# Up-projection's values in products of 256 columns, with ScalarE's bank copies put ahead of taps and GELU

## The chip, the cores and the metric

One core of one Trainium2 chip. The metric is the device time of one execution in microseconds (us). The profile is one execution recorded by the hardware profiler. Its engines are TensorE (PE, with its weight loads shown as PEld), VectorE (DVE), ScalarE (ACT), GpSimd (POOL) and SyncE (SP, which issues the large DMAs).

## The reference

A trunk of two layers over 512 tokens of 1024 features. The change lies in the gated MLP that both layers have:

```python
def _conv_ffn(h, w_up, conv_w, conv_b, w_down):
    u = _causal_depthwise_conv(h @ w_up, conv_w) + conv_b
    gate, up = jnp.split(u, 2, axis=-1)
    return (jax.nn.gelu(gate, approximate=False) * up) @ w_down

def reference(x, p, positions, ...):
    for i in range(DEPTH):
        ...
        x = x + _conv_ffn(_rms_norm(x, ffn_norm[i]), ffn_w_up[i], ffn_conv_w[i], ffn_conv_b[i], ffn_w_down[i])
        x = x + _per_layer_embedding(x, p[i], ple_norm[i], ple_w_gate[i], ple_w_proj[i])
    return x
```

`w_up` is 1024 x 5632: the first 2816 columns are the gate, the others the values (`up`). The convolution is causal, depthwise and three taps wide. Everything is float32.

## The kernel before

**Numbers as pairs.** Each float32 operand is split into a high part of a shorter type (`float32r`) and a low part, the rest. ScalarE writes the high part (`Copy` into `wh`, or `uh`, `a`, `four`), then VectorE subtracts it to get the low part (`wl`, `ul`). For weights this is `cut` (L146 on ScalarE, L147 on VectorE) or `cut_blocks` (L822, L823); for activations `split` (L105, L106). A product then is three matmuls: high by high, high by low, low by high (`mm3`, L166 to L168; in the block products L875 to L877). Features lie on the 128 partitions, the 512 tokens along the free dimension, so a full product is 512 columns wide and fills one PSUM bank of 512 float32. Eight blocks of 128 features (`xg[0]` to `xg[7]`, pairs) make up the contraction.

**One group.** `ffn` runs over 11 groups `d` in each layer. A group computes two blocks of 128 value columns and two blocks of 128 gate columns.

The two value blocks are plain products in `value` (L950): 8 blocks of the contraction by 3 matmuls, 512 columns wide, into one bank each (`ps` of `begin`, called the late value, and `V0`). Their weights are cut by `column` (L947, with `cut`) and lie at the start of their tiles.

The two gate blocks are computed by `seven` (L860), with seven block products in place of eight: contraction, columns and tokens are each halved, weights and activations are added and subtracted beforehand (`first_forms`, `more_forms`; for the activations `operand`), and seven products of 256 tokens, 12 matmuls each, are accumulated into the right halves of banks. Their weights come from `cut_blocks`, which puts the high parts 16 and the low parts 48 elements into a tile (`BLOCKS`). What one bank has in common with another is carried over by copies of ScalarE between banks: W's left half into X and Y (L886, L887), V into `more` in SBUF (L893), Y's left half to X's right (L896) and X's right half to Y's right (L900). `seven` is a generator; each `yield` is a place where TensorE is given value products, so that a copy can be made meanwhile.

TensorE's order is written out by hand (`manual_schedule`, L1039). For a group it is:

| run | matmuls | columns | what must be there |
|---|---|---|---|
| late value, blocks 0 to 5 | 18 | 512 | weights of value 1 |
| W | 12 | 256 | `plain` |
| late value, blocks 6 and 7 | 6 | 512 | |
| V | 12 | 256 | `t13` |
| X left | 12 | 256 | copy L886 |
| Y left | 12 | 256 | copy L887, `t` |
| V0, blocks 0 to 3 | 12 | 512 | weights of value 0 |
| X right | 12 | 256 | copy L896 |
| V0, blocks 4 to 7 | 12 | 512 | |
| Y left (`last`) | 12 | 256 | copy L900, `last` |
| X right (`last`) | 12 | 256 | |

That is 48 matmuls of 512 columns and 84 of 256. In the first group, the norm's transposes stand after each half of V0.

**After the products.** Each of the four banks goes through `taps` (L923): VectorE multiplies by the norm's scale `R` (L926; for Y, which first has `more` added, L929 and L932), ScalarE makes the middle tap with the bias (L933), VectorE adds the two other taps (L935, twice). ScalarE's GELU over both gate blocks (L1064) and VectorE's product with the values (L976 or L986, in `place`) end the group. These lines of group d are traced after `prepare(d + 1)` and `begin(d + 1)`, so they run while TensorE is in group d + 1. Their order on ScalarE and VectorE isn't written out: the scheduler places them, by traced order and its own estimates. From group 4 on, earlier results are split in between (`split_one`). ScalarE and VectorE each work through their instructions in order; one that waits holds up all behind it.

**Buffers.** `wh` and `wl` have three buffers each, the raw weights (1 MB DMAs on SP's queue, two for a group) two, the banks of kind `pa` (W, V, values) four, those of kind `ps` (X, Y) four. A weight cut must wait until the product that used its buffer three cuts earlier is over.

After the last group, `down` (L1091) multiplies by `w_down`; its first cuts are traced by `pump(0)` (L1195).

Of the kernel before, what the change touches and what calls it, by code (L numbers as in the profile page):

```python
# [1 line left out]

# [1 line left out]

# [14 lines left out]
P = 128  # L19
# [36 lines left out]


BLOCKS = (16, 48)


class Kernel:
# [64 lines left out]
        t = self.wp.tile([P, 2048], F32, tag="raw", name=self.nm("raw"), bufs=2)  # L126
        return t[:, : na * nb].rearrange("p (a b) -> p a b", b=nb)

    def cut(self, rv, by):


        nc = self.nc
        na, nb = rv.shape[1:]
        parts = []
        n = 2 if na * nb > 1024 else 1
        for k in range(n):
            if by == "b":
                a, b = na, nb // n
                v = rv[:, :, k * b : (k + 1) * b]
            else:  # L140
                a, b = na // n, nb
                v = rv[:, k * a : (k + 1) * a, :]
            h, l = self.weight_tiles()
            hv = h[:, : a * b].rearrange("p (a b) -> p a b", b=b)
            lv = l[:, : a * b].rearrange("p (a b) -> p a b", b=b)
            nc.scalar.activation(hv, v, AF.Copy)  # L146
            nc.vector.tensor_tensor(lv, v, hv.bitcast(F32), ALU.subtract)  # L147
# [12 lines left out]
        return get  # L160
# [699 lines left out]
    def seven(self, od, ws, xg, forms, keep=True):  # L860
# [35 lines left out]
        nc.scalar.copy(X[:, right], Y[:, left])  # L896
        yield
        last = self.cut_blocks(od)
        product(X[:, right], t13, 1, s3)
        nc.scalar.copy(Y[:, right], X[:, right])  # L900
        yield
        product(Y[:, left], last, 1, s4)
        product(X[:, right], last, 0, tokens(1, 1))
        yield X, Y, more
# [1 line left out]
    def ffn(self, i, project, next_gain):  # L906
# [8 lines left out]
        with tc.tile_pool(name=f"ffn{i}", bufs=1) as fp:  # L915
# [4 lines left out]
            def both():  # L920
                return fp.tile([P, 2, S], F32, tag="zt", name=self.nm("zt"), bufs=2)

            def taps(y, ps, f, more=None):  # L923
                z = fp.tile([P, S], F32, tag="z", name=self.nm("z"), bufs=3)
                if more is None:
                    nc.vector.tensor_tensor(z, ps, R, ALU.mult)  # L926
                else:
                    h2 = lambda x: x.rearrange("p (u t) -> p u t", u=2)
                    nc.vector.tensor_tensor(  # L929
                        h2(z), h2(ps), more.unsqueeze(1).to_broadcast([P, 2, S // 2]), ALU.add  # L930
                    )
                    nc.vector.tensor_tensor(z, z, R, ALU.mult)  # L932
                nc.scalar.activation(y, z, AF.Identity, scale=w2[:, f : f + 1], bias=bb[:, f : f + 1])  # L933
                for tap, w in ((1, w1), (2, w0)):
                    nc.vector.scalar_tensor_tensor(  # L935
                        out=y[:, tap:], in0=z[:, : S - tap], scalar=w[:, f : f + 1], in1=y[:, tap:],
                        op0=ALU.mult, op1=ALU.add,
                    )
# [6 lines left out]
                return out  # L945

            def column(raw, c):  # L947
                return self.cut(raw[:, :, c * P : (c + 1) * P], "b")

            def value(w, ps, k0, k1):  # L950
                for k in range(k0, k1):
                    self.mm3(ps, w(k, 0, P), xg[k], start=k == 0, stop=k == ND - 1)

            def prepare(d):

# [82 lines left out]
            steps, w1c, w0c = ready  # L1038
            with tc.manual_schedule(engines={ET.PE}):  # L1039
                late = begin(0, steps, w1c)  # L1040
                for d in range(groups):
                    g, y = both(), both()
                    next(steps)
                    V0 = self.pa()
                    value(w0c, V0, 0, ND // 2)
                    if d == 0:
                        self.end_norm()
                    next(steps)
                    value(w0c, V0, ND // 2, ND)
                    if d == 0:  # L1050
                        R = self.spread()
                    X, Y, more = next(steps)
                    rest = late

                    if d + 1 < groups:
                        steps, w1c, w0c = prepare(d + 1)
                        late = begin(d + 1, steps, w1c)
                    else:
                        split_acts()
                    rest(y)  # L1060
                    taps(y[:, 0], V0, NF + 2 * d)
                    taps(g[:, 0], X, 2 * d)
                    taps(g[:, 1], Y, 2 * d + 1, more)
                    nc.scalar.activation(g, g, AF.Gelu)  # L1064
                    place(d, g, y)
                    if 4 <= d < groups - 1:
                        split_one(d - 4)
            self.begin_norm(mine)
            finish = lambda m: self.advance(m, next_gain)
            if i == 1:  # L1070
# [14 lines left out]
            self.down(i, acts, down_forms, both, work, finish)  # L1085
            if i == 0:
                self.end_norm()
            else:
                self.ple1(fp)

    def down(self, i, acts, forms, both, work, finish):  # L1091


        nc, tc = self.nc, self.tc
# [96 lines left out]
        with tc.manual_schedule(engines={ET.PE}):  # L1191
            with tc.high_priority(offset=300):
                for _ in range(2):
                    load(loads.pop(0))
                pump(0)  # L1195
            for t, (u, name, k0, k1, s) in enumerate(plan):
                own = u not in banks
                if own:
# [778 lines left out]
```

## Time and profile before

| | |
|---|---|
| median of 3 runs | 1205.41 us (1204.26 to 1207.05) |
| the profiled execution: time, span | 1205.4 us, 1203.6 us |
| first value product of layer 0, of layer 1 | at 178.36 us, at 798.47 us |
| first product of the down-projection after each | at 406.80 us, at 1027.25 us |
| TensorE's granted clock, both stretches | 1.00 |

The two up-projections with their block products take 228.4 and 228.8 us, 38% of the span. A matmul's record in the trace lasts longer than the distance to the next one's start, since matmuls are pipelined; what TensorE really spends is read from start to start. In the view of lines and in the timeline, each row names engine, line, operation, tiles written and read (buffer numbers left out) and shape; in brackets stands how long its engine had been idle and what ended that.

### The profile page before, as it was taken

Reading aid. Unit: us, or ns where it says so; the run is one execution under the profiler, and the core shown is the slowest. Engines: PE = TensorE matmul, PEld = TensorE weight load, DVE = VectorE, ACT = ScalarE, POOL = GpSimd, SP = SyncE. Lnnn points to the kernel's source line nnn. Section 1 sums busy time; section 2 is a strip of 40 time slices with the busy share of each in tenths; the row PEclk is TensorE's granted clock in tenths of the full one; section 3 lists DMA queues with packets and bytes.
Section 4 is the critical chain, followed back from the end, with each engine's and each line's share of the span. In section 5 each row is a group of like instructions: output and inputs, shape, how many; then the busy total and the mean of one; then the engine's idle time right before and its main releaser. Section 6 shows DMA issues by size and latency. Waiting matters only on the chain.

```text
span 1203.6 us, 17728 instructions
## 1 busy us (share of the span) xinstructions
PE 1196.3 (99%) x7018; PEld 1036.0 (86%) x7018; DVE 968.4 (80%) x1543; ACT 665.5 (55%) x1093; POOL 44.7 (4%) x64
## 2 busy tenths in 40 slices
PE   9999999999999999999999999999999999999998
PEld 8877789998899889888988988889998898888887
DVE  6786687899999987746679876678999998978595
ACT  7466565656465643534563654555565555645374
POOL 2600000000000000000100000000000000000000
PEclk9999999999999999999999999999999999999999
DMA  7232222424232332232322222323242423322601
GB/s 222 74 102 72 74 71 72 139 71 138 74 122 89 119 121 89 93 105 82 111 93 70 74 68 70 106 74 102 72 139 70 141 70 124 131 88 97 210 1 70
DMA packets 111127, 117.61 MB, mean 98 GB/s; under 512 B 2840, under 2 KB 106322, under 8 KB 111044
## 3 DMA queue, kind: packets, MB, share of 16 engines
q1 hardware_dynamic: 109680, 115.35, 29.4%
q8 instruction: 55, 0.90, 0.3%
q0 software_dynamic: 560, 0.42, 0.3%
q10 hardware_dynamic: 804, 0.70, 0.2%
q14 instruction: 28, 0.23, 0.1%
HBM read 114.37 MB, written 2.10 MB: 97 GB/s over the span
## 4 chain that ended last, share of the span: by engine, by line
PE 82%; DVE 12%; DMA 2%; ACT 2%; issue 1%; ACTq 0%; DVEq 0%
PE ps L166 14%; PE ps L167 14%; PE ps L168 14%; PE pa L167 5%; PE pa L166 5%; PE pa L168 5%; PE ps L875 4%; PE ps L877 4%; PE ps L876 4%; DVE zt L935 3%; DMA raw<-in_ffn_w_up_dram 2%; DVE wl L823 2%; PE pa L875 2%; PE pa L877 2%; PE pa L876 2%; DVE wl L147 1%
## 5 line engine op out<-in xcount | busy, mean ns | idle before, releaser
L146 ACT ACTIVATE wh<-raw 128x1024 fp32r<-128x1024 f32 (+4 forms) x154 | 152.3, 991 | 141.7 <-PE ps L167 101.3
L147 DVE TENSOR_TENSOR wl<-raw,wh 128x1024 fp32r<-128x1024 f32 (+4 forms) x154 | 175.1, 1138 | 52.9 <-ACT wh L146 52.3
L822 ACT ACTIVATE wh<-raw 128x1024 fp32r<-128x1024 f32 x78 | 82.8, 1061 | 120.6 <-DVE raw L847 65.4
L935 DVE SCALAR_TENSOR_TENSOR zt<-z,vfa,zt 128x510 f32<-128x510 f32 (+1 forms) x176 | 130.7, 744 | 11.7 <-ACT zt L933 11.2
L823 DVE TENSOR_TENSOR wl<-raw,wh 128x1024 fp32r<-128x1024 f32 x78 | 95.3, 1222 | 24.3 <-ACT wh L822 24.2
L933 ACT ACTIVATE zt<-z,vfb 128x512 f32<-128x512 f32 x88 | 71.0, 809 | 29.4 <-DVE four L986 12.8
L166 PE MATMUL ps<-b,wh 128*128 128x512 f32 x192 | 76.7, 399 | 0.0
L167 PE MATMUL ps<-b,wh 128*128 128x512 f32 x192 | 75.1, 391 | 0.0
L168 PE MATMUL ps<-b,wl 128*128 128x512 f32 x192 | 75.0, 391 | 0.0
L167 PE MATMUL pa<-b,wh 128*128 128x512 f32 x176 | 69.0, 392 | 0.0
L167 PE MATMUL pa<-a,wh 128*128 128x512 f32 x176 | 69.0, 392 | 0.0
L166 PE MATMUL pa<-a,wh 128*128 128x512 f32 x176 | 69.0, 392 | 0.0
L166 PE MATMUL pa<-b,wh 128*128 128x512 f32 x176 | 69.0, 392 | 0.0
L168 PE MATMUL pa<-a,wl 128*128 128x512 f32 x176 | 68.4, 389 | 0.0
L168 PE MATMUL pa<-b,wl 128*128 128x512 f32 x176 | 68.4, 389 | 0.0
L875 PE MATMUL ps<-four,wh 128*128 128x256 f32 x232 | 65.3, 282 | 0.7 <-ACT ps L896 0.7
L877 PE MATMUL ps<-four,wl 128*128 128x256 f32 x232 | 64.4, 278 | 0.0
L876 PE MATMUL ps<-four,wh 128*128 128x256 f32 x232 | 64.2, 277 | 0.0
L166 PE MATMUL ps<-a,wh 128*128 128x512 f32 x160 | 63.6, 398 | 0.0
L167 PE MATMUL ps<-a,wh 128*128 128x512 f32 x160 | 62.4, 390 | 0.0
L168 PE MATMUL ps<-a,wl 128*128 128x512 f32 x160 | 62.4, 390 | 0.0
L166 PE MATMUL ps<-uh,wh 128*128 128x512 f32 x128 | 50.3, 393 | 0.0
(472 smaller groups left out, 3495.6 us busy)
## 6 DMA issues: line engine op xcount, KB each, us to landing
raw<-in_ffn_w_up_dram SPq DMA_DIRECT2D x44, 1024.0 KB, 5.1
raw<-in_ffn_w_down_dram SPq DMA_DIRECT2D x13, 1024.0 KB, 4.8
raw<-in_hy_w_in_dram SPq DMA_DIRECT2D x8, 1024.0 KB, 5.2
raw<-in_gla_w_in_dram SPq DMA_DIRECT2D x8, 1024.0 KB, 5.1
raw<-in_ffn_w_down_dram SPq DMA_DIRECT2D x8, 768.0 KB, 4.2
raw<-in_ple_w_gate_dram SPq DMA_DIRECT2D x6, 1024.0 KB, 4.7
raw<-in_hy_w_out_dram SPq DMA_DIRECT2D x16, 256.0 KB, 4.0
raw<-in_gla_w_out_dram SPq DMA_DIRECT2D x4, 1024.0 KB, 4.8
```

Of the source, the lines that this page charges most:

```text
L146: nc.scalar.activation(hv, v, AF.Copy)
L147: nc.vector.tensor_tensor(lv, v, hv.bitcast(F32), ALU.subtract)
L166: mm(out, lh, rh, start=start, stop=False, **kw)
L167: mm(out, lh, rl, start=False, stop=False, **kw)
L168: mm(out, ll, rh, start=False, stop=stop, **kw)
L822: nc.scalar.activation(h, src, AF.Copy)
L823: nc.vector.tensor_tensor(l, src, h.bitcast(F32), ALU.subtract)
L875: mm(out, wh, xh, start=first and j == 0, stop=False, **kw)
L876: mm(out, wh, xl, start=False, stop=False, **kw)
L877: mm(out, wl, xh, start=False, stop=j == ND // 2 - 1, **kw)
L933: nc.scalar.activation(y, z, AF.Identity, scale=w2[:, f : f + 1], bias=bb[:, f : f + 1])
L935: nc.vector.scalar_tensor_tensor(out=y[:, tap:], in0=z[:, : S - tap], scalar=w[:, f : f + 1], in1=y[:, tap:], op0=ALU.mult, op1=ALU.add,)
```

## The change

Four edits, of which the first three belong to the value products and their order:

1. `value` runs over the left and the right half of the tokens, 256 columns each, and over the contraction within each half: 2112 matmuls of 256 columns in place of 1056 of 512. Only the very first opens the bank's accumulation.
2. `column` puts the values' weights at the offsets of the block products (`BLOCKS`). The tiles had room for that already.
3. The copies L896 and L900 are handed out by the generator, and `issue_after` orders later instructions of ScalarE behind them: GELU, product and split of group d - 1 (now `close`, traced one step later, behind L896's copy of group d), the late value's taps (behind L900's copy), and the down-projection's first cut (behind the last L900 copy).
4. `taps` orders Y's multiply by `R` (L932) on VectorE behind the low part of the last cut made by then (`rest_cut`: the second value block of the next group).

```diff
+HALVES = (slice(0, S // 2), slice(S // 2, S))
...
-            h, l = self.weight_tiles()
+            h, l = self.weight_tiles(offs)
...
-            nc.vector.tensor_tensor(lv, v, hv.bitcast(F32), ALU.subtract)
+            self.rest_cut = nc.vector.tensor_tensor(lv, v, hv.bitcast(F32), ALU.subtract)
...
-        nc.scalar.copy(X[:, right], Y[:, left])
-        yield
+        yield nc.scalar.copy(X[:, right], Y[:, left])
...
-        nc.scalar.copy(Y[:, right], X[:, right])
-        yield
+        yield nc.scalar.copy(Y[:, right], X[:, right])
...
-                    nc.vector.tensor_tensor(z, z, R, ALU.mult)
+                    with tc.issue_after(behind.ins) if behind else nullcontext():
+                        nc.vector.tensor_tensor(z, z, R, ALU.mult)
...
-                return self.cut(raw[:, :, c * P : (c + 1) * P], "b")
+                return self.cut(raw[:, :, c * P : (c + 1) * P], "b", BLOCKS)
...
-                for k in range(k0, k1):
-                    self.mm3(ps, w(k, 0, P), xg[k], start=k == 0, stop=k == ND - 1)
+                for c, k in itertools.product(HALVES, range(k0, k1)):
+                    self.mm3(
+                        ps[:, c], w(k, 0, P), [x[:, c] for x in xg[k]], start=c.start == 0 and k == 0,
+                        stop=k == ND - 1,
+                        skip_group_check=True,
+                    )
...
                 late = begin(0, steps, w1c)
+                close = lambda: None
                 for d in range(groups):
                     g, y = both(), both()
-                    next(steps)
+                    copied = next(steps)
+                    with tc.issue_after(copied.ins):
+                        close()
                     V0 = self.pa()
                     value(w0c, V0, 0, ND // 2)
...
-                    next(steps)
+                    copied = next(steps)
                     value(w0c, V0, ND // 2, ND)
...
-                    rest = late
+                    rest, cut = late, None
                     if d + 1 < groups:
                         steps, w1c, w0c = prepare(d + 1)
+                        cut = self.rest_cut
                         late = begin(d + 1, steps, w1c)
                     else:
                         split_acts()
-                    rest(y)
+                    with tc.issue_after(copied.ins):
+                        rest(y)
                     taps(y[:, 0], V0, NF + 2 * d)
                     taps(g[:, 0], X, 2 * d)
-                    taps(g[:, 1], Y, 2 * d + 1, more)
-                    nc.scalar.activation(g, g, AF.Gelu)
-                    place(d, g, y)
-                    if 4 <= d < groups - 1:
-                        split_one(d - 4)
+                    taps(g[:, 1], Y, 2 * d + 1, more, cut)
+
+                    def close(d=d, g=g, y=y):
+                        nc.scalar.activation(g, g, AF.Gelu)
+                        place(d, g, y)
+                        if 4 <= d < groups - 1:
+                            split_one(d - 4)
+
+                close()
...
-                pump(0)
+                with tc.issue_after(copied.ins):
+                    pump(0)
```

The built program has the same instructions as before on ScalarE, VectorE, GpSimd and SyncE, in another order on the first two within the up-projections and just behind them; GpSimd's and SyncE's orders are the same. TensorE has 1056 matmuls more, each with its weight load.

More of the change, by code (lines that the diff above doesn't have):

```diff
@@ L1 @@
-from contextlib import ExitStack
+import itertools
+from contextlib import ExitStack, nullcontext
 import numpy as np
@@ L127, in raw, with cut @@
         return t[:, : na * nb].rearrange("p (a b) -> p a b", b=nb)
-    def cut(self, rv, by):
+    def cut(self, rv, by, offs=(0, 0)):
         nc = self.nc
@@ L921, in both, with taps @@
                 return fp.tile([P, 2, S], F32, tag="zt", name=self.nm("zt"), bufs=2)
-            def taps(y, ps, f, more=None):
+            def taps(y, ps, f, more=None, behind=None):
                 z = fp.tile([P, S], F32, tag="z", name=self.nm("z"), bufs=3)
@@ L1084, in ffn @@
                 split_pair(f)
-            self.down(i, acts, down_forms, both, work, finish)
+            self.down(i, acts, down_forms, both, work, finish, copied)
             if i == 0:
@@ L1089, in ffn, with down @@
                 self.ple1(fp)
-    def down(self, i, acts, forms, both, work, finish):
+    def down(self, i, acts, forms, both, work, finish, copied):
         nc, tc = self.nc, self.tc
```

## The prediction

> **What bounds the kernel now.** I read the page's busy table first, then the chain that ended last, then the stretches of the two up-projections, and then the starts of single matmuls.
>
> ```profile
> span 1203.6 us, 17728 instructions
> PE 1196.3 (99%) x7018; PEld 1036.0 (86%) x7018; DVE 968.4 (80%) x1543; ACT 665.5 (55%) x1093; POOL 44.7 (4%) x64
> ...
> PE 82%; DVE 12%; DMA 2%; ACT 2%; issue 1%; ACTq 0%; DVEq 0%
> ```
>
> TensorE is busy for 99% of the span and makes up 82% of the chain, so only what it does between two starts can be won. Its records overlap (a matmul is booked for 0.28 or 0.40 us, yet the next one starts much sooner), so I count from start to start. These rows are the first product of each run of one group of the up-projection (columns: start, duration, engine, line, tiles). The first and last are the starts of two successive groups.
>
> ```profile
> 261.59 0.40 PE L166 MATMUL pa<-a,wh 128*128 128x512 f32 x1
> ...
> 265.69 0.28 PE L875 MATMUL pa<-a,wh 128*128 128x256 f32 x1
> ...
> 267.07 0.40 PE L166 MATMUL pa<-a,wh 128*128 128x512 f32 x1
> ...
> 268.46 0.28 PE L875 MATMUL pa<-four,wh 128*128 128x256 f32 x1
> ...
> 269.84 0.28 PE L875 MATMUL ps<-a,wh 128*128 128x256 f32 x1
> ...
> 271.20 0.28 PE L875 MATMUL ps<-four,t 128*128 128x256 f32 x1
> ...
> 272.56 0.40 PE L166 MATMUL pa<-a,wh 128*128 128x512 f32 x1
> ...
> 275.31 0.28 PE L875 MATMUL ps<-four,wh 128*128 128x256 f32 x1
> ...
> 282.18 0.40 PE L166 MATMUL pa<-a,wh 128*128 128x512 f32 x1
> ```
>
> A run of twelve 256-wide products that follows another such run takes 271.20 - 269.84 = 1.36 us, and so does the next (to 272.56): 113.3 ns for each. Steady 512-wide products stand in the projection just before the first up-projection; six of them:
>
> ```profile
> 177.00 0.39 PE L166 MATMUL ps<-b,wh 128*128 128x512 f32 x1
> ...
> 178.36 0.39 PE L166 MATMUL pa<-a,wh 128*128 128x512 f32 x1
> ```
>
> That is 1.36 us for six, 226.7 ns for each: exactly two of 113.3. So a group of 48 products of 512 and 84 of 256 should take 48 x 0.2267 + 84 x 0.1133 = 20.40 us. It takes 282.18 - 261.59 = 20.59. The missing 0.19 us stands at the changes of width: the twelve 256-wide after a 512-wide run take 267.07 - 265.69 = 1.38 instead of 1.36, the six 512-wide after that 1.39 (to 268.46) instead of 1.36, the next twelve 1.38. A change between two 256-wide runs costs nothing, although one of these also changes the kind of PSUM bank (`pa` to `ps`, at 269.84) and the other the weight pool (`wh` to `t`, at 271.20). There are eight changes of width in a group: 0.19 / 8 = 24 ns for each.
>
> Some groups take longer. The starts of the second and the last group of each layer, and of what follows the last:
>
> ```profile
> 199.83 0.40 PE L166 MATMUL pa<-a,wh 128*128 128x512 f32 x1
> 386.21 0.40 PE L166 MATMUL pa<-a,wh 128*128 128x512 f32 x1
> 406.80 0.40 PE L166 MATMUL ps<-uh,wh 128*128 128x512 f32 x1
> 819.92 0.40 PE L166 MATMUL pa<-b,wh 128*128 128x512 f32 x1
> 1005.91 0.40 PE L166 MATMUL pa<-b,wh 128*128 128x512 f32 x1
> 1027.25 0.40 PE L166 MATMUL ps<-uh,wh 128*128 128x512 f32 x1
> ```
>
> The view of waits says what the long ones wait for, first for layer 0, then for layer 1 (the weight loader runs ahead of the matmuls, so its waits are longer than what TensorE loses):
>
> ```profile
> PEld ps L875 <- ACT ps L896: 0.9, 2, 0.7
> PEld ps L875 <- ACT ps L900: 0.4, 1, 0.4
> PEld ps L875 <- ACT ps L886: 0.2, 1, 0.2
> ...
> PEld ps L875 <- ACT ps L896: 1.3, 2, 0.7
> PEld ps L875 <- ACT ps L900: 0.3, 1, 0.3
> ```
>
> All are ScalarE's copies between banks. The longest of layer 0, in ScalarE's and TensorE's order of time:
>
> ```profile
> 313.87 1.06 ACT L822 ACTIVATE wh<-raw 128x1024 fp32r<-128x1024 f32 x1
> 316.01 1.06 ACT L1064 ACTIVATE zt<-zt 128x1024 f32<-128x1024 f32 x1 [1.08 <-DVE zt L935]
> 316.98 0.37 ACT L896 COPY ps<-ps 128x256 f32<-128x256 f32 x1
> ...
> 312.87 0.28 PE L875 MATMUL ps<-four,t 128*128 128x256 f32 x1
> 314.23 0.40 PE L166 MATMUL pa<-a,wh 128*128 128x512 f32 x1
> 317.40 0.39 PE L875 MATMUL ps<-four,wh 128*128 128x256 f32 x1 [0.26 <-ACT ps L896]
> ```
>
> The product that the copy reads was issued by 314.23, yet the copy starts at 316.98: the GELU (L1064) stands ahead of it and itself waits 1.08 us for VectorE's taps. The run from 314.23 takes 3.17 us, in the quiet group 275.31 - 272.56 = 2.75.
>
> **The change part by part.**
>
> *Value products in halves.* 2 layers x 22 columns x 8 x 3 = 1056 matmuls of 512 columns become 2112 of 256, each with its own weight load as now. Work: 2112 x 113.3 - 1056 x 226.7 ns = 0. That is the lower bound of their price; the upper one is the kernel's other 256-wide row, where the weights lie unshifted in their tile, near the end of the program:
>
> ```profile
> 1196.35 0.28 PE L1372 MATMUL ps<-wh,b 128*128 128x256 f32 x1
> ...
> 1199.10 0.28 PE L1374 MATMUL ps<-four,a 128*128 128x256 f32 x1
> ```
>
> 23 starts in 2.75 us: 119.6 ns. At that price the halves would cost 2112 x 6.3 ns = +13.3 us. I take the first: the change moves the values' weights to the offsets (16 and 48 elements) of the block products, and the moving operand is the same tile that block products already read in both halves (token halves of `xg`), at 113.3.
>
> For this same place the Trainium skill (TensorE: Matmul & The Clock Gate, section Back-to-back issue gap) has a rule against the change: a warm matmul takes N / 2.4 ns plus about 2.5 ns whatever its width, so each split would add 2.5 ns, 2.6 us over 1056, and the sum below would be 1201.8. The rows above show no such fixed part: twelve of 256 and six of 512 both take 1.36 us.
>
> *Changes of width.* Within a group all eight go. From the rows above, the time over 20.40 for each group is, for the nine from the second start to the last, 386.21 - 199.83 - 183.60 = 2.78 in layer 0 and 1005.91 - 819.92 - 183.60 = 2.39 in layer 1; for the last group 406.80 - 386.21 - 20.40 = 0.19 and 1027.25 - 1005.91 - 20.40 = 0.94. In each first group five changes go (its first run follows 512-wide work, and two runs end at the norm's transposes) and one is new (512-wide projection to 256-wide value): 4 x 0.024 = 0.10. Together 2.78 + 2.39 + 0.19 + 0.94 + 0.20 = 6.5 us. Of this, 20 x 0.19 + 0.2 = 4.0 belongs to the changes of width and 2.5 to the late copies.
>
> *Copies ahead of taps and GELU.* Nothing is added; ScalarE's order changes. In the built order a group now runs on ScalarE: L886's copy ahead of the cut of `t` (now behind it), ..., the fourth tap activation, L896's copy, a split, the GELU, the cut of the next group's first value weights, L900's copy, the next taps. On VectorE the multiply by R (L932) moves behind the cut of the second value weights, and the cut of `last` ahead of the last two taps, so the GELU comes later. VectorE's present rows give its steps from start to start:
>
> ```profile
> 312.18 0.68 DVE L932 TENSOR_TENSOR z<-z,R 128x512 f32<-128x512 f32 x1
> 312.79 1.21 DVE L147 TENSOR_TENSOR wl<-raw,wh 128x1024 fp32r<-128x1024 f32 x1
> 313.92 0.74 DVE L935 SCALAR_TENSOR_TENSOR zt<-z,vfa,zt 128x511 f32<-128x511 f32 x1
> 314.58 0.68 DVE L926 TENSOR_TENSOR z<-pa,R 128x512 f32<-128x512 f32 x1
> ```
>
> 0.61 for a multiply or a split, 1.13 for a cut, 0.66 for a tap. The cut in them ends at 314.00 and TensorE starts on it at 314.23: the thinnest margin. VectorE's work in a whole group, from the stretch over which layer 0 is steady (third busy column):
>
> ```profile
> 195.00:400.00 205.00, 204.74 (x1309) 184.25 (x1309) 190.15 (x253) 117.19 (x170) 0.00 (x0) 1.00 0.30 98
> ```
>
> 1309 / 132 = 9.92 groups, 19.17 us of work in each, 1.5 idle. In the new order VectorE waits once in a group for nothing else to do, for the GELU's 1.06: a loop of 19.17 + 1.06 = 20.23, which 20.40 just covers. I put this loop on TensorE's clock, zero at a group's start (261.59 above).
> - *Second value cut.* If the GELU ends at 15.1 (below), that is -5.3 for the next group. Between the cut and the GELU lie multiply, `last`, two taps and a split, 0.61 + 1.13 + 0.66 + 0.66 + 0.61 = 3.7, so 19.17 - 3.7 = 15.5 lie from the GELU to the cut's end: 10.2. Due at 10.9 (272.56 now is 10.97). Slack 0.7.
> - *L896's copy.* The multiply ends at 10.9, the activation (half a GELU's columns, so at most its 1.06) at 11.9, the copy (0.37) at 12.3. Due at 13.6. Slack 1.3, where now it is late.
> - *L900's copy.* `last` is cut on ScalarE once the run that ends at 271.20 (9.6) has let its buffer go: 10.7; on VectorE 1.13 to 11.9; taps and split 1.9 to 13.9; the GELU 15.0 to 15.1; the next cut (1.06) 16.2, the copy 16.6. Due at 17.7. Slack 1.1.
>
> So all three hold, on VectorE's loop, whose cover is 0.17 us a group: what it costs if that is gone stands under rival 2.
>
> Layer 1 has the same built order as layer 0, and SP's and POOL's queues keep theirs: no DMA is passed. The first cut of the down-projection is put behind the last group's L900 copy; its buffer comes free at the end of the very run that this copy reads, so it waits no longer. The rest of the program is as before.
>
> **Sum.** The profiled execution took 1205.4 us, its span 1203.6 and 1.8 around it; the median of the runs shown is 1205.41, the same. 1205.4 - 6.5 = 1198.9; I give back 0.3 of it to single groups in which VectorE's loop is fuller than its mean (an estimate: 0.17 us in two groups): 1199.2.
>
> **Rivals.**
> 1. *Slower: the halves run at the unshifted row's pace.* Mechanism: the right halves of the even `xg` tiles, which no block product reads today, or the values' weights, meet the loads as the 119.6 ns products do. For it: 6.3 ns is real in this trace. Against it: offsets and tiles are those of the 113.3 ns products. 1199.2 + 13.3 = 1212.5. It decides from 6.2 us / 2112 = 2.9 ns per product.
> 2. *VectorE becomes the bound.* If it goes on idling 1.5 us in each group, groups stay at 19.17 + 1.5 = 20.67, and the time at 1205. For it: it is 93% busy. Against it: the loop above has one wait only.
> 3. *Late copies stay, elsewhere.* L900 stands behind GELU and cut; if VectorE is 1 us later than I place it, the 2.5 us remain: 1201.7.
> 4. *The change of width isn't what costs the 24 ns*, but something else in the values, so that the change doesn't do what it says: only the copies gain, 1205.4 - 2.5 + 0.3 = 1203.2. Against it: bank and pool changes cost nothing in the rows.
> 5. *A fixed price of each matmul*, between the rows' 0 and 6.3 ns: with 2.5 for each of the 1056 added ones 1199.2 + 2.6 = 1201.8, still faster. Against it: the equal 1.36 us. (It is what the Trainium skill's rule quoted above would make of the halves.)
>
> **Chances and range.** Forecast 0.66, rivals in order 0.06, 0.05, 0.12, 0.07, 0.04. What a measurement of this kernel can tell from no change is about 0.2%, 2.4 us: faster means under 1203.0. Forecast, third and fifth lie below it, the fourth on it (counted half), the first above: faster 0.85, same 0.08, slower 0.07. The three runs before span 2.8 us, so the forecast's own range is 1197.6 to 1201.0; the whole range takes in rivals 3 to 5 and ends at 1203.6, with rivals 1 and 2 (0.11) left out.
>
> **What would show it.** Right: no 512-wide products between the first and last start of a layer's up-projection; 256-wide starts 113.3 ns apart throughout; groups of 20.40 us; no TensorE wait on the three copies there; VectorE's busy share of these stretches up by one point. Wrong: products 116 ns apart or more (rival 1); groups above 20.5 with VectorE without idle time (2); waits named L896's or L900's successors (3); the same 24 ns now between value and block runs (4).

## The result and the profile after

| | before | after |
|---|---|---|
| median | 1205.24 us (1204.26 to 1207.05, 6 runs) | 1210.68 us (1209.43 to 1213.59, 6 runs) |
| ratio to before | | 1.0044, 95% interval 1.0034 to 1.0055 |
| the profiled execution: time, span | 1205.4, 1203.6 us | 1212.2, 1210.4 us |
| up-projection of layer 0, of layer 1 | 228.4, 228.8 us | 232.0, 230.7 us |

The changed kernel is slower by 0.44%; 1199.2 was predicted. An up-projection is counted here and below from the start of its first value product to the start of the first product of the down-projection. Of the 6.8 us by which the profiled execution is longer, 5.5 lie in the two up-projections.

Lines of after that are used below stand at other numbers than in before: the products are L169 to L171 (`mm3`) and L878 to L880 (`seven`), a weight cut L149 and L150 (`cut`) or L825 and L826 (`cut_blocks`), the copies L896 (`more`), L899 and L902 (formerly L893, L896 and L900), the multiply with R L927 and L934, the other taps L937, GELU L1077, the loads of the raw weights L946.

The page's first rows and its chain:

```profile
span 1210.4 us, 19832 instructions
...
PE 1199.7 (99%) x8074; PEld 1080.0 (89%) x8074; DVE 968.3 (80%) x1543; ACT 667.0 (55%) x1093; POOL 45.1 (4%) x64
...
PE 63%; DVE 26%; DMA 7%; ACT 3%; issue 2%; ACTq 0%; DVEq 0%
```

TensorE is still booked as 99% busy, but it holds 63% of the chain instead of 82%; VectorE went from 12 to 26%, the DMAs from 2 to 7%. The starts of groups, in the view of time (start, duration, engine, line, tiles), show where. The rows are groups 0, 1, 2, 4 and 5 of layer 0 and the down-projection behind it:

```profile
179.01 0.28 PE L169 MATMUL pa<-a,wh 128*128 128x256 f32 x1
...
200.38 0.28 PE L169 MATMUL pa<-a,wh 128*128 128x256 f32 x1
...
220.78 0.28 PE L169 MATMUL pa<-a,wh 128*128 128x256 f32 x1
...
262.04 0.28 PE L169 MATMUL pa<-a,wh 128*128 128x256 f32 x1
...
283.68 0.28 PE L169 MATMUL pa<-a,wh 128*128 128x256 f32 x1
...
411.04 0.40 PE L169 MATMUL ps<-uh,wh 128*128 128x512 f32 x1
```

The first quiet group takes 220.78 - 200.38 = 20.40 us, the sum that was predicted for all of them. A later one takes 283.68 - 262.04 = 21.64, and the ten from the second start on 411.04 - 200.38 = 210.66, or 21.07 each. The view of waits names what TensorE's weight loader waited for in the whole program, and the stretch of the steady groups says whether VectorE is full (its columns: length; busy time and instructions of PE, PEld, DVE, ACT, POOL; granted clock, DMA share, GB/s):

```profile
PEld ps L878 <- ACT ps L902: 6.4, 11, 1.6
...
PEld pa L171 <- DVE wl L150: 2.3, 9, 0.3
...
PEld ps L880 <- DVE t L826: 1.2, 5, 0.3
...
195.00:400.00 205.00, 202.87 (x1753) 200.40 (x1753) 183.11 (x244) 113.85 (x163) 0.29 (x1) 1.00 0.28 94
```

The copy ahead of the last block products (L902, formerly L900) is now its longest wait in total, and weight cuts are late as well. Yet VectorE is busy for 183 us of the 205, where it was 190 before: it is not full, it waits. The waits of VectorE in the same stretch that end with ScalarE's half of a weight cut (total, times, longest):

```profile
DVE wl L150 <- ACT wh L149: 6.8, 8, 1.5
...
DVE wl L826 <- ACT wh L825: 3.5, 5, 1.5
```

The chain of waits from 270 to 325 us (start, duration, what) says for what:

```profile
273.94 1.15 DVE wl L826
...
275.10 8.21 DMA raw<-in_ffn_w_up_dram
...
283.40 1.07 ACT wh L825
...
294.31 1.23 DVE wl L150
...
295.55 5.54 DMA raw<-in_ffn_w_up_dram
...
301.17 1.07 ACT wh L149
...
315.26 1.22 DVE wl L150
...
317.07 1.15 DVE wl L826
...
318.24 8.00 DMA raw<-in_ffn_w_up_dram
```

No TensorE work stands in it. It goes in circles through the two buffers of raw weights. (A load's landing is counted from its issue until its data are there.) The cut of `last` (to 275.09) is the last reader of the gate weights; only then can the next group's be loaded into that buffer, and 8.21 us later their first cut (`plain`, 283.40) can begin. In the same way the cut of value column 0 (294.31) lets the value weights be loaded, and the cut of value column 1 (301.17) waits for them. From one release to the next lie VectorE's work in between and the landing of 1 MB. On ScalarE this has a second consequence:

```profile
299.29 1.06 ACT L1077 ACTIVATE zt<-zt 128x1024 f32<-128x1024 f32 x1 [1.48 <-DVE zt L937]
301.17 1.06 ACT L149 ACTIVATE wh<-raw 128x1024 fp32r<-128x1024 f32 x1 [0.82 <-DMA raw<-in_ffn_w_up_dram]
302.13 0.37 ACT L902 COPY ps<-ps 128x256 f32<-128x256 f32 x1
```

The value cut stands ahead of L902's copy. It waits for the DMA, and the copy, which needs nothing from it, waits behind.

### The profile page after: what moved, and what is told of

Its sections match the earlier page's. It is cut to its first block, busy times and chain, and to the rows that moved or that the text cites. A ratio compares the mean times of both kernels' runs of the same rounds, so it can differ in the third digit from the quotient of the medians.

```text
span 1210.4 us, 19832 instructions
## 1 busy us (share of the span) xinstructions
PE 1199.7 (99%) x8074; PEld 1080.0 (89%) x8074; DVE 968.3 (80%) x1543; ACT 667.0 (55%) x1093; POOL 45.1 (4%) x64
## 4 chain that ended last, share of the span: by engine, by line
PE 63%; DVE 26%; DMA 7%; ACT 3%; issue 2%; ACTq 0%; DVEq 0%
PE ps L169 13%; PE ps L171 13%; PE ps L170 13%; DMA raw<-in_ffn_w_up_dram 7%; DVE zt L937 6%; DVE wl L826 5%; DVE wl L150 4%; PE ps L878 2%; PE pa L171 2%; PE pa L170 2%; PE ps L880 2%; PE ps L879 2%; PE pa L169 2%; DVE z L927 2%; PE ps L1390 1%
## 5 line engine op out<-in xcount | busy, mean ns | idle before, releaser
L149 ACT ACTIVATE wh<-raw 128x1024 fp32r<-128x1024 f32 (+4 forms) x154 | 152.3, 991 | 140.3 <-PE ps L170 90.4
L150 DVE TENSOR_TENSOR wl<-raw,wh 128x1024 fp32r<-128x1024 f32 (+4 forms) x154 | 175.4, 1140 | 62.9 <-ACT wh L149 61.2
L825 ACT ACTIVATE wh<-raw 128x1024 fp32r<-128x1024 f32 x78 | 82.9, 1063 | 104.7 <-DVE raw L850 67.8
L937 DVE SCALAR_TENSOR_TENSOR zt<-z,vfa,zt 128x510 f32<-128x510 f32 (+1 forms) x176 | 131.1, 746 | 0.8
L826 DVE TENSOR_TENSOR wl<-raw,wh 128x1024 fp32r<-128x1024 f32 x78 | 95.4, 1223 | 16.1 <-ACT wh L825 15.8
L171 PE MATMUL pa<-b,wl 128*128 128x256 f32 x352 | 98.1, 279 | 0.3
L171 PE MATMUL pa<-a,wl 128*128 128x256 f32 x352 | 98.0, 279 | 0.3
L169 PE MATMUL pa<-a,wh 128*128 128x256 f32 x352 | 97.3, 276 | 0.0
L170 PE MATMUL pa<-a,wh 128*128 128x256 f32 x352 | 97.2, 276 | 0.0
L169 PE MATMUL pa<-b,wh 128*128 128x256 f32 x352 | 97.2, 276 | 0.0
L170 PE MATMUL pa<-b,wh 128*128 128x256 f32 x352 | 97.2, 276 | 0.0
L169 PE MATMUL ps<-b,wh 128*128 128x512 f32 x192 | 76.6, 399 | 0.0
L171 PE MATMUL ps<-b,wl 128*128 128x512 f32 x192 | 75.0, 390 | 0.0
L878 PE MATMUL ps<-four,wh 128*128 128x256 f32 x232 | 65.5, 283 | 3.1 <-ACT ps L902 2.9
L171 PEld LDWEIGHTS pa<-b,wl 128*128 128x128 f32 x352 | 66.1, 188 | 1.4 <-DVE wl L150 1.3
L171 PEld LDWEIGHTS pa<-a,wl 128*128 128x128 f32 x352 | 66.1, 188 | 1.2 <-DVE wl L150 1.0
L169 PEld LDWEIGHTS pa<-a,wh 128*128 128x128 f32 x352 | 66.1, 188 | 0.0
L169 PEld LDWEIGHTS pa<-b,wh 128*128 128x128 f32 x352 | 66.1, 188 | 0.0
L170 PEld LDWEIGHTS pa<-a,wh 128*128 128x128 f32 x352 | 66.1, 188 | 0.0
L170 PEld LDWEIGHTS pa<-b,wh 128*128 128x128 f32 x352 | 66.1, 188 | 0.0
```

What stands on the lines that cost most here:

```text
L150: self.rest_cut = nc.vector.tensor_tensor(lv, v, hv.bitcast(F32), ALU.subtract)
L169: mm(out, lh, rh, start=start, stop=False, **kw)
L170: mm(out, lh, rl, start=False, stop=False, **kw)
L171: mm(out, ll, rh, start=False, stop=stop, **kw)
L825: nc.scalar.activation(h, src, AF.Copy)
L826: nc.vector.tensor_tensor(l, src, h.bitcast(F32), ALU.subtract)
```

## The experiments

All times are medians; the ratio is to the kernel before, timed on the same chip, with its 95% interval. (The kernel before had 1205.97 us beside e1 to e5, 1205.48 beside e6 to e9 and 1205.22 beside e10 to e13.) The last columns are the up-projections of the profiled execution.

| run | time, us | ratio | layer 0 | layer 1 |
|---|---|---|---|---|
| e1_halves_only | 1214.42 | 1.0068 (1.0055 to 1.0080) | 232.0 | 232.9 |
| e2_order_only | 1203.81 | 0.9981 (0.9971 to 0.9990) | 227.3 | 227.3 |
| e3_no_multiply_order | 1208.69 | 1.0021 (1.0012 to 1.0030) | 229.5 | 228.5 |
| e5_halves_unshifted | 1215.17 | 1.0077 (1.0065 to 1.0090) | 234.2 | 233.2 |
| e6_after_own | 1208.56 | 1.0026 (1.0015 to 1.0037) | 230.9 | 230.1 |
| e7_halves_own | 1212.59 | 1.0056 (1.0042 to 1.0069) | 232.0 | 230.7 |
| e8_before_own | 1204.94 | 0.9996 (0.9987 to 1.0005) | 228.5 | 228.2 |
| e9_no_multiply_own | 1204.37 | 0.9994 (0.9985 to 1.0003) | 228.0 | 227.3 |
| e10_after_split | 1200.65 | 0.9961 (0.9948 to 0.9975) | 225.8 | 225.8 |
| e11_halves_split | 1206.09 | 1.0006 (0.9997 to 1.0014) | 228.4 | 228.2 |
| e12_before_split | 1204.31 | 0.9991 (0.9983 to 1.0000) | 227.5 | 227.4 |
| e13_no_multiply_split | 1200.79 | 0.9962 (0.9949 to 0.9974) | 225.8 | 225.8 |

### First: which part of the change costs

**The halves alone.** The kernel before with these lines (shortened; `...` marks the end of a cut line) and nothing of the new order:

```
-        return self.cut(raw[:, :, c * P : (c + 1) * P], "b")
+        return self.cut(raw[:, :, c * P : (c + 1) * P], "b", BLOCKS)
-        for k in range(k0, k1):
-            self.mm3(ps, w(k, 0, P), xg[k], start=k == 0, stop=k == ND - 1)
+        for c, k in itertools.product(HALVES, range(k0, k1)):
+            self.mm3(ps[:, c], w(k, 0, P), [x[:, c] for x in xg[k]], ...
```

> The kernel before with the halved values and the block placement of their weights alone; ScalarE's and VectorE's order is left as it was. Theory A (the new order of ScalarE and VectorE costs: the second value column's cut frees the raw buffer, its reload takes some 5.6 us, the next cut stands ahead of the copy, and this loop takes 20.9 us instead of 20.4): without the new order the time falls by the width changes, so 1205.2 - 4 = 1201 us, ratio 0.995 to 0.998, and the quiet groups of TensorE take 20.40 us. Theory B (the halves themselves cost, since a faster TensorE exposes VectorE's queue whatever the order): ratio 1.003 or more, groups over 20.6 us. Theory C (halving and placement do nothing): 1.000.

Measured: 1214.42, ratio 1.0068. My theory A, that the new order costs, fell with this run: the new order is not in it, and it is slower than the whole change. (The built order isn't quite that of before: in the steady groups ScalarE's is the same, but on VectorE the scheduler put one multiply with R ahead of a cut instead of behind it; in the first groups more differs.) Theory B was right in its sign. But TensorE's products aren't slower, and VectorE is no fuller than before (186 of 205 us busy). The chain of waits shows the loop through the gate weights' buffer, group after group:

```profile
256.51 4.86 DMA raw<-in_ffn_w_up_dram
...
276.80 6.43 DMA raw<-in_ffn_w_up_dram
...
298.66 5.08 DMA raw<-in_ffn_w_up_dram
...
319.16 5.13 DMA raw<-in_ffn_w_up_dram
...
339.99 5.53 DMA raw<-in_ffn_w_up_dram
```

From one load to the next: 20.29, 21.86, 20.50 and 20.83 us. Less the landing, that is 15.43, 15.43, 15.42 and 15.70: nearly always the same work of ScalarE and VectorE, between the landing of one group's gate weights and the last cut of them, and a landing of 4.9 to 6.5 us on top. So the loop takes 20.3 to 21.9 us. A TensorE group of 20.59 leaves 20.59 - 15.43 = 5.16 for the landing, one of 20.40 only 4.97 us, and four of these five landings are longer than that.

**The order alone.** The changed kernel with the two lines of `value` and that of `column` as they were before.

> The changed kernel with its value products of 512 columns and unshifted weights again: only the new order of ScalarE and VectorE is left. Theory A: the order costs by itself, ratio 1.002 to 1.007 (2.5 to 8 us slower), and the waits of TensorE for the copies of the last block product and the late landing of the weights are there as in the changed kernel; the groups take 20.8 to 21 us. Theory B (the halves expose it): with a group of 20.59 us the order is free or gains up to 2.5 us, ratio 0.998 to 1.000.

Measured: 0.9981, every group but each layer's first 20.59 us, and the up-projections 228.43 + 228.78 - 227.33 - 227.32 = 2.6 us shorter than before. The second theory holds: the new order gains, and by the 2.5 us that the prediction gave to the late copies. (Here too the scheduler moved something with the width: one copy of ScalarE, L890, and one multiply of VectorE stand elsewhere in each steady group than in the changed kernel.)

**Without the last step of the order.**

```
-                    with tc.issue_after(behind.ins) if behind else nullcontext():
-                        nc.vector.tensor_tensor(z, z, R, ALU.mult)
+                    nc.vector.tensor_tensor(z, z, R, ALU.mult)
```

> The changed kernel without the last step of its order: the multiply with R on the second gate column no longer waits for the second value cut; the taps and GELU stay behind the copies. If that step holds the loop (it takes 1.2 us out of the time in which the weights are under way and puts it behind them): ratio 0.997 to 1.000, groups near 20.4 to 20.6. If the taps behind the copies hold it (two y1 taps of 1.5 us go from before the first value cut to behind it): about the changed kernel's time, ratio 1.003 to 1.006.

Measured: 1.0021, between the two cases. Without that wait the kernel is 2 to 3 us faster than with it. Its chain still goes through the reloads, one in each group. So this step, with the few other places that the scheduler changed along with it, decides only part of it.

**The placement.** The first kernel without `BLOCKS` in `column`.

> The first of these kernels (halves alone, order of before) with the value weights at the start of their buffers instead of 16 and 48 elements in. If the placement decides the pace as the one row of unshifted 256-wide products has it (119.6 ns against 113.3): 2112 products, 6.3 ns each, 13 us more than the kernel with placement, less what the groups' waits absorb: 1208 to 1215 us. If placement does nothing: the same time as the kernel with it, within 1 us.

Measured: 1215.17, only 0.75 us over the kernel with placement. Read by the totals, placement would do nothing. The starts of groups 1 and 2 of layer 0, and between them those of a value run, of the block run behind it and of the next run, say otherwise:

```profile
200.32 0.28 PE L169 MATMUL pa<-a,wh 128*128 128x256 f32 x1
...
206.01 0.28 PE L169 MATMUL pa<-a,wh 128*128 128x256 f32 x1
...
207.45 0.28 PE L878 MATMUL pa<-four,wh 128*128 128x256 f32 x1
...
208.83 0.28 PE L878 MATMUL ps<-a,wh 128*128 128x256 f32 x1
...
221.41 0.28 PE L169 MATMUL pa<-a,wh 128*128 128x256 f32 x1
```

A quiet group takes 21.09 us instead of 20.40; 14 of the 20 later groups take just that. Spread over its 96 half products this is 0.69 / 96 = 7.2 ns for each. But it isn't all in them: twelve value products take 207.45 - 206.01 = 1.44 us, 120 ns each, near the 119.6 of the prediction's row, and the twelve block products behind them take 1.38 instead of 1.36, though every product here has 256 columns. At 21.09 TensorE is slow enough for nearly all of the reloads; at 20.40 the waits give back what the placement gains.

### Second: is it the reload

**A third buffer.** Up to group 8 one tile of the kind `four` is still unused; the gate weights of groups 1 to 8 go there, and the two raw buffers are left to the values.

```
+                if 1 <= d <= 8 and not own:
+                    own.append(self.four(fp, F32).rearrange("p a b -> p (a b)").rearrange("p (a b) -> p a b", b=256))
-                out = [self.raw(ND, 256) for _ in range(2)]
+                out = [self.raw(ND, 256), own[0] if 1 <= d <= 8 else self.raw(ND, 256)]
```

> The changed kernel, with a third buffer for the raw up-projection weights in groups 1 to 8 of each layer (a tile of the fours that is not needed until then), so that the value and the gate weights no longer share two buffers. Theory A (the loop of cut, 1 MB reload and next cut, 20.9 to 21 us, holds the groups above TensorE's 20.40 us): the waits go in the groups with the third buffer, these take 20.40 to 20.5 us, the two up-projections fall by 4 to 6 us each, the time is 1199 to 1202 us, ratio 0.994 to 0.997. Theory B (VectorE's own 19.2 us of work with its waits for ScalarE, or the copy behind the cut on ScalarE, hold it, whatever the buffers): the groups stay at 20.9 to 21 us, the ratio at 1.003 to 1.005.

> The halves with their placement in the order of before, with the same third buffer. Here the chain runs from the last cut of the block products over the reload to the plain cut: 15.4 us of VectorE and ScalarE, and 4.9 to 6.5 us of landing. Theory A: with a buffer of its own the gate weights' reload still waits for the last cut, but lands alone in about 5.0 us: 20.4 to 20.5 us for each group, so up-projections of 225.5 to 227.5 us instead of 232 and 233, time 1202 to 1205 us, ratio 0.997 to 1.000. Theory B: 1214 us as without the buffer, ratio 1.006 to 1.008.

> The kernel before with the third buffer alone. Theory A: the loop is just under TensorE's 20.59 us there and reaches over it in single groups (20.82, 21.37, 21.17 us); with the buffer all of the groups 1 to 8 take 20.59 us, and 1.0 to 2.5 us go, ratio 0.998 to 0.999. Theory B: these groups wait for something else, ratio 1.000.

> The changed kernel without its wait of the multiply with R for the second value cut, with the third buffer. Theory A: as with that wait, groups of 20.40 to 20.5 us where the buffer is, 1199 to 1201 us, ratio 0.994 to 0.997; the order then makes less than 2 us of difference between this kernel and the one with the wait. Theory B: groups of 20.6 to 20.9 us as without the buffer, ratio 1.002.

Measured: 1208.56, 1212.59, 1204.94 and 1204.37. All four are misses for theory A as I had put it in numbers: some 2 us gained against the kernel without the buffer in the first two where 9 to 12 were expected, no difference to before in the third, and 4.3 us in the fourth where 8 to 10 were. By their times alone the first three are nearer to theory B. The chain of the first shows why a buffer more wasn't enough:

```profile
253.49 7.01 DMA four<-in_ffn_w_up_dram
...
274.47 7.53 DMA four<-in_ffn_w_up_dram
...
295.98 7.55 DMA four<-in_ffn_w_up_dram
...
317.50 6.49 DMA four<-in_ffn_w_up_dram
```

The value loop is off the chain, since the value weights are now loaded a group ahead. The gate loop is left: it has one buffer still. From load to load it is 20.98, 21.51 and 21.52 us, so the work in it is 13.97, 13.98 and 13.97, 1.45 shorter than in the order of before. But the landing is 6.5 to 7.6 us: the value load is issued 1.74 us ahead of it, and both are under way together (the last section sets landings beside such distances). One buffer more opens one of the two loops and leaves the other closed.

**Smaller loads.** Of each pair of columns one is cut at once and the other several us later. So the load is divided:

```
-                for raw, c0 in zip(out, (DFF + 256 * d, 256 * d)):
-                    nc.sync.dma_start(raw, wu[:, :, c0 : c0 + 256])
+                for u, c in ((0, 1), (1, 0), (0, 0), (1, 1)):
+                    c0 = (DFF + 256 * d, 256 * d)[u] + c * P
+                    nc.sync.dma_start(out[u][:, :, c * P : (c + 1) * P], wu[:, :, c0 : c0 + P])
```

In the built order the two halves of a tile stand together on SP's queue, the one that is cut first ahead.

> The changed kernel with each 1 MB load of raw up-projection weights issued as two of 512 KB by column, those first that are cut first: value column 1, gate columns 0, value column 0, gate columns 1. No buffer is added. Theory A (the loop through the reload holds the groups): what the next cut waits for lands in 3 to 5 us instead of 5.1 to 8.2, the loops fall to 18 to 20 us, and the groups go to TensorE's 20.40 us: up-projections of 225.5 to 228 us instead of 232.0 and 230.7, time 1199 to 1203 us, ratio 0.995 to 0.998. Rival (the landing is set by the 2 MB that go together or by a fixed time for each transfer, not by the size of one): landing stays above 5 us, ratio 1.002 to 1.006.

> The halves with their placement, in the order of before, with the same loads of 512 KB. Theory A: the loop of 15.4 us and the landing comes to 18.5 to 20 us, so the groups take 20.40 us but for the waits of the order of before (the copies behind the taps, 0.4 us at a time): time 1199 to 1204 us, ratio 0.995 to 0.999. Rival: 1212 to 1215 us as without, ratio 1.006.

> The kernel before with the loads of 512 KB alone. Theory A: only the groups of before that were over 20.59 us (20.82, 21.37, 20.72, 21.17) can gain, so 0.5 to 2.5 us, ratio 0.998 to 0.9995. Rival: ratio 1.000 or above, since eight loads of 512 KB cost the queue more than four of 1 MB.

> The changed kernel without its wait of the multiply with R for the second value cut, with the loads of 512 KB. Theory A: groups of 20.40 to 20.5 us throughout, up-projections of 225.5 to 227 us, time 1198 to 1201 us, ratio 0.993 to 0.997. Rival: 1208 us as without, ratio 1.002.

Measured: 1200.65, 1206.09, 1204.31 and 1200.79. The whole change with divided loads is faster than both kernels: by 0.39% than before, and by some 10 us than the change alone. Its chain from 225 to 395 us, summed by line, and then the starts of groups 1 and 2, of group 10 and of the down-projection:

```profile
by line: PE pa L171 17.6%; PE pa L169 17.5%; PE pa L170 17.5%; PE ps L880 11.3%; PE ps L878 11.3%; PE ps L879 11.2%; PE pa L879 4.6%; PE pa L880 4.6%; PE pa L878 4.6%
```

```profile
199.24 0.28 PE L169 MATMUL pa<-a,wh 128*128 128x256 f32 x1
...
219.64 0.28 PE L169 MATMUL pa<-a,wh 128*128 128x256 f32 x1
...
383.26 0.28 PE L169 MATMUL pa<-a,wh 128*128 128x256 f32 x1
...
403.67 0.40 PE L169 MATMUL ps<-uh,wh 128*128 128x512 f32 x1
```

The chain consists of products alone, and the groups take 20.40 us again: group 1, the last one and all others behind the first, but for two in each layer, which take 20.55 to 20.67. Nothing but these loads differs from the changed kernel; ScalarE, VectorE and GpSimd run the same instructions in the same order. So its loss is shown to lie in the reload. What I expected of the landing itself was off. ScalarE's waits for the raw weights between 195 and 400 us, in the changed kernel and in this one:

```profile
ACT wh L825 <- DMA raw<-in_ffn_w_up_dram: 9.2, 8, 1.9
...
ACT wh L149 <- DMA raw<-in_ffn_w_up_dram: 6.6, 7, 1.7
```

```profile
ACT wh L825 <- DMA raw<-in_ffn_w_up_dram: 6.1, 6, 1.8
```

The value cut (L149) no longer waits, the gate cut waits less. The loads of 512 KB land 3.6 to 7.7 us after their issue, not 3 to 5. The loops need not be as short as I had thought; it is enough that TensorE no longer waits for them.

The third and fourth of these runs fit this: the kernel before gains 0.9 us, at the edge of the noise (the interval ends at 1.0000), its two long groups in layer 0 (20.82 and 21.37) go to 20.71 and 20.59, and the step of the order that cost 2 us without divided loads now costs nothing. The second is a miss: in the order of before, the halves only come to the time of before. Its groups from group 7 on take 20.40 us, but those from 2 to 6 go up to 21.7. Its chain there has two reloads left in layer 0, in an order whose work was 1.45 us longer with loads of 1 MB; whether that makes up all of the difference was not taken apart. The order, which took 2.6 us out of the up-projections at 512 columns, takes 228.42 + 228.23 - 225.80 - 225.78 = 5.1 out of them with halves and divided loads.

## Why the prediction was wrong

**The step that failed** is the loop of VectorE: "In the new order VectorE waits once in a group for nothing else to do, for the GELU's 1.06: a loop of 19.17 + 1.06 = 20.23, which 20.40 just covers", together with "no DMA is passed". The loop has other waits, for the raw weights, because it is closed by their buffers: last cut, reload, first cut of the next group. The order of the DMAs was indeed kept; the time at which they can be issued was not looked at. In the steady stretch VectorE idles 205 - 183.1 = 21.9 us over 205 / 21.07 = 9.7 groups, 2.25 in each where I had 1.06. The waits for the GELU add up to 6.0 + 5.9 us there, 1.2 in each group, near what I had. The waits for the weight cuts shown above add up to 6.8 + 3.5, 1.1 in each group, where I had nothing. As a loop: the work of 13.97 in the new order, read from the run with the third buffer, and the changed kernel's landings of 6.2 to 8.2 for the gate weights make 20.2 to 22.2; in the order of before, work of 15.4 and a landing of 4.9 to 6.5 make 20.3 to 21.9. Either way nearly the whole of it lies above the 20.40 that the halves bring. In before it can be estimated at 15.43 and the landings of 5.0 to 5.2 us shown at the end, 20.4 to 20.6: just under TensorE's 20.59, so the 0.19 us that the change takes away was about the room there was.

By the sum: the ten later groups of each layer took 210.66 us in layer 0 and 209.34 in layer 1 (worked out from the starts in the same way), where 204.0 were forecast for each. That is 12.0 us for which the prediction had 0.3. The other 1.3 us of the miss of 13.0 in the profiled execution lie ahead of the first up-projection and behind the second, 0.65 in each.

**The slacks** of 0.7, 1.3 and 1.1 us. L899's copy (formerly L896) held: its waits are gone. The cut of the second value weights and L902's copy, with 0.7 and 1.1, did not, since they were worked out in a loop that had no landing in it. That the first value cut stands ahead of L902's copy was written down ("the GELU 15.0 to 15.1; the next cut (1.06) 16.2, the copy 16.6"), but the cut was taken to have its weights. Where the reloads are out of the way, the working holds: in groups 4 to 8 of layer 0 L902's copy starts 16.0 to 16.3 us after its group with the divided loads, near the forecast, and 17.3 to 18.5 in the changed kernel.

**The halves at no cost, and the placement**: right. The quiet groups take 20.40 = 180 x 113.3 ns, and without placement a half product takes 120 ns, where 119.6 was read from the only such row of before. So rival 1 fell for the reason given, though its 1212.5 comes nearest to the measured 1210.68: that is chance, for the products of the changed kernel's quiet groups run at 113.3 ns. Rival 5 fell with the same 20.40. The Trainium skill (TensorE: Matmul & The Clock Gate, section Back-to-back issue gap) has 2.5 ns on top of a matmul's columns, but for a single matmul by itself, which the prediction left out; for the 48 added in a group it would be 0.12 us, and no quiet group shows it.

**The changes of width**: their time is gone as forecast, so rival 4's price fell, but its doubt didn't. In the kernel before, every change of width is also a change between unshifted and shifted weights, and the halves and the placement went in together. In the run without placement all products have 256 columns, and a block run behind a value run still takes 1.38 us instead of 1.36. So at least part of the 24 ns comes with the change of place; no run has shifted weights at 512 columns, and the shares stay open.

**The width of 4.0 us and the copies of 2.5**: right, where the reloads allow them. The order alone takes 2.6 us out of the up-projections, and the divided loads with halves and order another 227.33 + 227.32 - 225.80 - 225.78 = 3.1; the 20.55 to 20.67 us of two groups in each layer, 0.8 in all, make up nearly the rest of the 4.0. So 1200.65 was reached, near the 1199.2 forecast, but by a kernel with an edit that I hadn't seen to be needed.

**Rival 3** (late copies stay, elsewhere, 1201.7) had its sign come true: L900's successor L902 is the copy that TensorE's weight loader waits for. Its condition was met too: in group 5 of layer 0 the GELU ends at 300.35 - 283.68 = 16.7 where 15.1 was forecast, and the value cut behind it then waits 0.82 us more. But both come from the reloads, which the rival doesn't speak of, and the price is several times its 2.5 us.

**Rival 2** (VectorE the bound, 1205) was nearest in mechanism, at a chance of 0.05. It missed the place, for it spoke of VectorE's idle time of before going on, and the price, for the idle time grew. The row that spoke for it was quoted in the prediction: 190 of 205 us busy, 1.5 us idle in each group. I took that idle time to be free, without looking at what ended it. A third of those 14.9 us, 5.2, ends with ScalarE's half of the gate weights' cut, which in its turn waits for the load (waits of before, from 195 to 400 us):

```profile
ACT wh L822 <- DMA raw<-in_ffn_w_up_dram: 9.7, 7, 1.9
...
DVE wl L823 <- ACT wh L822: 5.2, 7, 1.4
```

The loop stood in the trace of before.

## What to carry to other kernels

A buffer that is filled by a DMA makes a loop: from its last reader over the reload to its first reader and on to the last again; its period is that work plus the landing, and it limits the kernel as an engine does, though no engine in it is full. Before the bounding engine is made faster, work out the period of every such loop; the one that lies just below is the next bound, and a change of order that brings two last readers close together can lengthen the landings too, as they were longer here. A part that the totals show to be worth nothing may be worth its full gain once that bound is lifted; look at the quiet groups for it. And where one edit changes two things at the same places, here width and place of the weights, their shares need a run that changes only one.

## What the runs showed of the hardware

The landing of 1 MB goes with what else is under way. For the raw weights at one place of the program, before and after (rows of the view of a tile: issues, with duration in ns and first and last start, and the time to landing):

```profile
L944 SPq DMA_DIRECT2D raw<-in_ffn_w_up_dram x1: 368/368/368, 272.4 to 272.4; - x1
DMA to landing us min/median/max: 5.0/5.0/5.0
...
L944 SPq DMA_DIRECT2D raw<-in_ffn_w_up_dram x1: 368/368/368, 275.5 to 275.5; - x1
DMA to landing us min/median/max: 5.2/5.2/5.2
```

```profile
L946 SPq DMA_DIRECT2D raw<-in_ffn_w_up_dram x1: 368/368/368, 273.4 to 273.4; - x1
DMA to landing us min/median/max: 6.0/6.0/6.0
...
L946 SPq DMA_DIRECT2D raw<-in_ffn_w_up_dram x1: 368/368/368, 275.1 to 275.1; - x1
DMA to landing us min/median/max: 8.2/8.2/8.2
```

Issued 3.1 us apart, the two loads land after 5.0 and 5.2 us; issued 1.7 us apart, after 6.0 and 8.2. The other pairs of the up-projections go the same way: in the changed kernel the second load of all nine pairs that its trace has 1.74 us apart lands after 6.2 to 8.2 us, in the kernel before that of seven of the eight pairs 3.05 us apart after 4.9 to 5.5, of one after 6.4. The Trainium skill (DMA: Bandwidth & Descriptors, section Issuing engines are not separate DMA queues) says that DMAs run on the same 16 engines and interleave there, whichever engine started them; these landings agree with it. No run varied the distance alone.

The place of the values' weights in their tile is worth some 6.7 ns for each product of 256 columns (120 against 113.3 ns), 0.69 us a group with what the block runs behind them lose. Runs of 512 columns with unshifted weights in turn with runs of 256 with shifted ones cost 0.19 us a group (20.59 against 20.40 us). Why, and how much of this is width and how much place, no run here shows.
